# The back half of the delta rule for two groups of heads, 8 matrices, at once

## The chip, the cores and the metric

The kernel runs on one core of a Trainium2 chip. Its metric is device time in microseconds; before, the median of three runs is 2629.19 us (2629.15 to 2630.71). The engines are TensorE (PE in the trace; its weight loads are PEld), VectorE (DVE), ScalarE (ACT), GpSimd (POOL) and SyncE (SP), each with its own instruction stream that runs in program order; they wait for each other by semaphores.

## The reference, cut to what matters

The trunk has two layers over 256 tokens of width 2048 in float32: a gated DeltaNet mixer and MLP, then an indexer-sparse attention and MLP. The change is in the first mixer. In the reference it is, for each of 32 heads and each chunk of tokens:

```python
l_mat = where(strict, (k * beta) @ k.T * decay, 0)
t_mat = triangular_solve(eye + l_mat, eye)          # (1 + L)^-1
u, w = t_mat @ (v * beta), t_mat @ (k * beta * exp(gc))
v_new = u - w @ state
o = (q * exp(gc)) @ state + where(lower, q @ k.T * decay, 0) @ v_new
o = rms_norm(o, out_norm) * silu(z)                 # the norm and the gate
return o.reshape(b, t, 4096) @ w_out
```

## The kernel before, in words

The kernel holds tokens in two blocks of 128 instead of the reference's chunks of 64. A head has one matrix L of 128x128 for each block; the second block takes a correction from the first.

**Main work.** Every weight is loaded by SyncE in items of 512 KB, and `Stream.get` splits each item into two float32r parts (`whi` by ScalarE, `wlo` by VectorE), three items ahead of its use. A product is three matmuls (`mm3`). For each of 16 groups `g` (two value heads, one key head) the main loop makes the projection of k, q, v (`by_channel`, 192 matmuls of 128x256), then that of the gate z (`by_token`, 96 more). After the 16 groups, `two_chunks` starts the output projection, which leaves the last four heads to its end.

**Background work.** The delta rule of a group is a generator, `delta(g, s, zg)`, of some 30 dependent steps. The front half makes convolution, SiLU, the products `pk` of k with k and q, and the masked matrices `la`. The back half is:
- `Lc`, `Lm`, `Tc`, `Tct`: diagonal blocks of 32, inverted by doubling in four levels (lines 599 to 612). A level is a run of 32x32 matmuls, a ScalarE copy to `Pm`, a second run, and VectorE's subtraction and transpose.
- two merges, from blocks of 32 to 64 (32x32 matmuls, lines 617 to 636) and from 64 to 128 (64x64 matmuls, `T64`, `P64`, lines 638 to 646), into `Tt`.
- solve, correction and solve (`r`, `yv`, lines 649 to 665), and the output `o` (lines 667 to 677).
- the norm: four small VectorE steps on `so`, then the inverse root `f` as 13 small GpSimd instructions (line 687); the gate (line 691), four transposes (`aux<-wide,r`), and the split into `hT` (line 700), which marks ("o", 2g) and ("o", 2g+1) as ready.

**What sets the order.** The order on each engine is fixed when the program is built. `Background` interleaves: after each three or four products of the main work `tick` emits steps of at most three active generators, each when a rough account of the engines' times (`Pace`) says that its inputs should be there. `ensure(key)` is the exception: while a key is not ready it emits the oldest generator's steps one after the other, with no main work between them. It stands at line 350 and 370 (an input of the next matmul), at 707, and before the gate tile `zg`, of which there are three:

```python
713            if g > 2:
714                ensure(("o", 2 * g - 6))
```

A generator also waits by itself: line 534 holds `pk` back until the output of group g-2 is ready, since the tiles have two buffers.

On TensorE every float32 matmul is two records in the trace, and a transpose is one; the order below shows instructions, so a run of 16 there is 32 records.

Of the kernel before, what the change touches and what calls it, by code (L numbers as in the profile page):

```python
# [7 lines left out]
F32 = mybir.dt.float32  # L8
F32R = mybir.dt.float32r
I32 = mybir.dt.int32  # L10
AF = mybir.ActivationFunctionType
# [3 lines left out]
P = 128  # L15
# [12 lines left out]
class Pace:  # L28
    """A rough account of when each engine gets through what it has been given, in microseconds."""
# [98 lines left out]
class Stream:  # L128
    """The weights in the order of their use: loaded, and split into two float32r parts, ahead of it."""
# [40 lines left out]
def tile_hybrid_trunk(ctx: ExitStack, tc: tile.TileContext, a: dict, out: bass.AP):  # L170
# [170 lines left out]
    def by_channel(n_items, part, key, n_ct=4, ahead=0):  # L341
        """Channels on partitions: [128 channels, 256 tokens] each, two to a bank."""
# [16 lines left out]
    def by_token(n_items, part, key, n_cols=512, outs=None, k0=0):  # L359
        """Tokens on partitions: [128 tokens, n_cols] for each of the two blocks of tokens."""  # L360
# [17 lines left out]
    def two_chunks(tiles, key, nk):  # L378
        """The first two blocks of columns of a mixer's output, which leave the last heads to the end."""
# [78 lines left out]
    with tc.tile_pool(name="delta", bufs=2, reuse_waits="tile") as dp:  # L458
        gl_dram = dramp.tile([DN_H, T], F32, name="gl_dram")

# [40 lines left out]
        def delta(g, s, zg):  # L501
# [32 lines left out]
            while g > 1 and ("o", 2 * g - 4) not in ready:  # L534
                yield
# [23 lines left out]
            units = [(i, b) for i in range(2) for b in range(2)]  # L559
            line = lambda x: x.rearrange("p i b c -> p (i b c)")  # L560
            rows = lambda q, n=1: slice(B * q, B * (q + n))
            Lc = dp.tile([P, 4, B], F32, name="Lc")
            Lm = dp.tile([P, len(LEVELS), 4, B], F32, name="Lm")
            Tc = dp.tile([P, 4, B], F32, name="Tc")
            Tct = dp.tile([P, 4, B], F32, name="Tct")
            Pm = dp.tile([P, 4, B], F32, name="Pm")
            Tt = dp.tile([P, 2, 2, P], F32, name="Tt")
            pool.memset(Tt, 0.0)
            la = (dp.tile([P, 2, 2, T], F32, name="la0"), dp.tile([P, 2, 2, P], F32, name="la1"))
            for b, n, o in ((0, T, 0), (1, P, T)):  # L570
                for i in range(2):
                    e = E[:, i, o:o + n].unsqueeze(1).to_broadcast([P, 2, n])
                    dve.scalar_tensor_tensor(la[b][:, i], e, wj[:, 2 * i + b:2 * i + b + 1], pk[b], op0=OP.mult, op1=OP.mult)
            for b in range(2):
                for q in range(4):
                    act.copy(Lc[rows(q), b::2], la[b][rows(q), :, 0, rows(q)])
# [6 lines left out]
            r = dp.tile([P, 2, 2, P], F32, name="r")  # L583
            for b in range(2):
                act.activation(r[:, :, b], t[:, :, b], AF.Copy, scale=nk[:, b:b + 1])
# [4 lines left out]
            each = lambda x: x.unsqueeze(1).to_broadcast([P, 4, B])  # L590
# [3 lines left out]
            dve.transpose(Tc.rearrange("p u c -> p (u c)"), Tct.rearrange("p u c -> p (u c)"))  # L594
            pool.tensor_tensor(Lm, Lc.unsqueeze(1).to_broadcast([P, n_l, 4, B]),
                               fine[:, 2:].unsqueeze(2).to_broadcast([P, n_l, 4, B]), op=OP.mult)
            yield True
            small_bank = lambda: aux()[:, 0:4 * B].rearrange("p (u c) -> p u c", u=4)
            for n in range(n_l):
                t = small_bank()  # L600
                for u in range(4):
# [5 lines left out]
                for u in range(4):  # L607
# [3 lines left out]
                dve.transpose(Tct.rearrange("p u c -> p (u c)"), Tc.rearrange("p u c -> p (u c)"))  # L611
                yield
            fold = Lm.rearrange("p n u c -> p (n u c)")
            T64 = fold[:, 0:256].rearrange("p (u c) -> p u c", u=4)
            P64 = fold[:, 256:512].rearrange("p (u c) -> p u c", u=4)
            Ttu = Tt.rearrange("p i b c -> p (i b) c")
            t = small_bank()
            for u, (i, b) in enumerate(units):
# [11 lines left out]
            for u in range(4):  # L630
# [7 lines left out]
            t = aux()[:, 0:256].rearrange("p (u c) -> p u c", u=4)  # L638
            for u, (i, b) in enumerate(units):
# [3 lines left out]
            t = aux()[:, 0:256].rearrange("p (u c) -> p u c", u=4)  # L643
            for u in range(4):
# [3 lines left out]
            # y = T r, with what the first block takes from the second's r  # L648
            yv = dp.tile([P, 2, 2, P], F32, name="yv")
# [10 lines left out]
            for i in range(2):  # L660
                pe.matmul(t[:, i * P:i * P + P], lhsT=la[0][:, i, 0, P:T], rhs=yv[:, i, 0], start=True, stop=True)
            dve.tensor_tensor(r[:, :, 1], r[:, :, 1], t[:, :T].rearrange("p (i d) -> p i d", i=2), op=OP.subtract)
# [3 lines left out]
            # o, its norm and its gate  # L666
            t = aux().rearrange("p (i b d) -> p i b d", i=2, b=2)
            for i in range(2):
                pe.matmul(t[:, i, 0], lhsT=la[0][:, i, 1, 0:P], rhs=yv[:, i, 0], start=True, stop=True)
                pe.matmul(t[:, i, 1], lhsT=la[0][:, i, 1, P:T], rhs=yv[:, i, 0], start=True, stop=False)  # L670
                pe.matmul(t[:, i, 1], lhsT=la[1][:, i, 1, :], rhs=yv[:, i, 1], start=False, stop=True)
            so = small_tile(4, "so")
            o = fold.rearrange("p (i b c) -> p i b c", i=2, b=2)
            act.copy(line(o), line(t))
            for i, b in units:
                act.activation(yv[:, i, b], o[:, i, b], AF.Square, accum_out=so[:, 2 * i + b:2 * i + b + 1])
            yield
            sc = small_tile(2, "sc")
            s2 = small_tile(2, "s2")
            f = small_tile(4, "f")  # L680
            pair = lambda x: x.rearrange("p (i b) -> p i b", i=2)
            rep = lambda x: x.unsqueeze(1).to_broadcast([P, 2, 2])
            dve.tensor_scalar(sc, rs[:, 2:4], 0.25 * float(P ** -0.5), None, op0=OP.mult)
            dve.scalar_tensor_tensor(s2, sc, 4.0 / P, sc, op0=OP.mult, op1=OP.mult)
            dve.tensor_tensor(pair(so), pair(so), rep(s2), op=OP.mult)
            dve.tensor_scalar(so, so, EPS, None, op0=OP.add)
            rsqrt(f, so, 4, pool)
            pool.tensor_tensor(pair(f), pair(f), rep(sc), op=OP.mult)
            yield True
            for i, b in units:  # L690
                dve.scalar_tensor_tensor(r[:, i, b], o[:, i, b], f[:, 2 * i + b:2 * i + b + 1], zg[:, b, i * P:i * P + P],
                                         op0=OP.mult, op1=OP.mult)
            yield
            t = aux()
            for i, b in units:
                pe.transpose(t[:, (2 * i + b) * P:(2 * i + b + 1) * P], r[:, i, b], ident)
            if g % 2 == 0:
                hT.append(h_pair())
            at = slice(2 * (g % 2), 2 * (g % 2) + 2)
            split(t, hT[g // 2][0][:, at].rearrange("p n t -> p (n t)"), hT[g // 2][1][:, at].rearrange("p n t -> p (n t)"), vec("out"))  # L700
            ready.update({("o", 2 * g), ("o", 2 * g + 1)})
# [33 lines left out]
    def chunk_done(outs, c, key, gain, scale=None, last=True):  # L735
        """A block of 512 columns of the residual stream; where it is final, what the next layer takes."""
# [62 lines left out]
    with tc.tile_pool(name="dsa", bufs=1, reuse_waits="tile") as sp, ExitStack() as late:  # L799
# [15 lines left out]
        def q_latent():  # L815
            # 1/sqrt(mean(q^2) + eps) of q = rstd*u is rsqrt(mean(u^2) + eps/rstd^2)/rstd
# [228 lines left out]
```

## Time and profile before

| | |
|---|---|
| median of 3 runs | 2629.19 us |
| profiled execution, span | 2626.4 us |
| TensorE busy | 2588.8 us (99%) |
| VectorE busy | 1546.4 us (59%) |
| ScalarE busy | 1292.3 us (49%) |
| GpSimd busy | 331.1 us (13%) |
| DeltaNet layer, about | 60 to 860 us of the span |
| idle time of TensorE there, named waits | 1.5, 1.0, 0.7, 0.6 and 0.3 us |

The profiled execution's own time is its span; what lies around it in a timed run is taken as the difference to the median, 2.8 us. A busy share says how long an engine had an instruction in it, and TensorE's matmuls overlap, so that its share is read with the spacing of the starts. Times in the timeline are from the span's start, and "x32" means that 32 instructions in a row of one kind are one line.

### The profile page before, as it was taken

The page shows a single profiled execution, that of the slowest core. Times are in us where ns is not written, and L with a number is a line of the kernel's source. Part 1 is how long each engine was busy: PE and PEld are TensorE (multiplying, and loading weights), DVE is VectorE, ACT ScalarE, POOL GpSimd, SP SyncE. Part 2 cuts the span into 40 slices and gives each one's busy share as a digit, 9 for nine tenths or more (in the row PEclk, how much of TensorE's full clock was granted, in tenths as well). Part 3 has the DMA queues.
Part 4 walks back from the last instruction along what each step waited for, and adds up shares of the span by engine and source line. Part 5 has one row for each costly group of instructions (what it writes and reads, how often), then busy time and mean ns, then how long its engine had stood idle before and what let it go on. Part 6 is the DMA issues. An engine that isn't in the chain of part 4 may idle for free.

```text
span 2626.4 us, 52946 instructions
## 1 busy us (share of the span) xinstructions
PE 2588.8 (99%) x21827; PEld 2362.0 (90%) x21827; DVE 1546.4 (59%) x2313; ACT 1292.3 (49%) x1995; POOL 331.1 (13%) x674
## 2 busy tenths in 40 slices
PE   7999999999999999999999999999999999999997
PEld 7999999999987899988899988898899988999886
DVE  5777676676764555554455554586555544455544
ACT  4555555555554444443344444566544433444443
POOL 0344444343431000000000000000000000000000
PEclk9999999999999999999999999999999999999999
DMA  6655455555554566666666666643666666666664
GB/s 191 186 147 141 137 150 139 149 146 147 144 168 153 182 189 195 194 193 193 193 186 186 190 190 188 181 133 120 179 191 194 193 195 194 189 188 187 192 193 137
DMA packets 325394, 455.95 MB, mean 174 GB/s; under 512 B 18280, under 2 KB 159840, under 8 KB 324768
## 3 DMA queue, kind: packets, MB, share of 16 engines
q1 hardware_dynamic: 321888, 443.85, 56.8%
q10 hardware_dynamic: 2928, 7.37, 0.8%
q8 instruction: 171, 2.80, 0.4%
q0 software_dynamic: 336, 1.34, 0.1%
q14 instruction: 71, 0.58, 0.1%
HBM read 450.37 MB, written 2.13 MB: 172 GB/s over the span
## 4 chain that ended last, share of the span: by engine, by line
PE 66%; DVE 1%; ACT 0%; issue 0%; ACTq 0%; DVEq 0%
PE acc L78 64%; PE aux L78 1%; PE pk L78 1%; DVE wlo L78 0%; DVE score L78 0%; ACT whi L78 0%; DVE p L78 0%; DVE m L78 0%; ACT acc L78 0%; DVE qtl L78 0%; DVE nm L78 0%; ACT h L78 0%; DVE h L78 0%; DVE rs_t L78 0%; DVE rs_u L78 0%
## 5 line engine op out<-in xcount | busy, mean ns | idle before, releaser
L78 DVE TENSOR_TENSOR wlo<-raw,whi 128x1024 fp32r<-128x1024 f32 x842 | 1029.6, 1229 | 868.4 <-ACT whi L78 861.3
L78 ACT CAST whi<-raw 128x1024 fp32r<-128x1024 f32 x842 | 878.3, 1049 | 853.3 <-PE acc L78 820.7
L78 PE MATMUL acc<-whi,h 128*128 128x512 f32 x2816 | 886.0, 392 | 2.1 <-ACT acc L78 2.1
L78 PE MATMUL acc<-xhi,whi 128*128 128x256 f32 x3088 | 875.9, 284 | 0.3 <-ACT whi L78 0.3
L78 PE MATMUL acc<-xhi,wlo 128*128 128x256 f32 x3088 | 860.5, 279 | 0.5 <-DVE wlo L78 0.5
L78 PE MATMUL acc<-xlo,whi 128*128 128x256 f32 x3088 | 860.8, 279 | 0.0
L78 PEld LDWEIGHTS acc<-whi,h 128*128 128x128 f32 x2816 | 528.7, 188 | 112.2 <-ACT acc L78 2.9
L78 PEld LDWEIGHTS acc<-xhi,wlo 128*128 128x128 f32 x3088 | 585.1, 189 | 0.8 <-DVE wlo L78 0.8
L78 PEld LDWEIGHTS acc<-xhi,whi 128*128 128x128 f32 x3088 | 581.3, 188 | 4.6 <-ACT whi L78 0.7
L78 PEld LDWEIGHTS acc<-xlo,whi 128*128 128x128 f32 x3088 | 581.8, 188 | 0.2
L78 PE MATMUL acc<-wlo,h 128*128 128x512 f32 x1408 | 548.3, 389 | 0.0
L78 PEld LDWEIGHTS acc<-wlo,h 128*128 128x128 f32 x1408 | 264.5, 188 | 52.7
L78 PE MATMUL acc<-whi,xhi 128*128 128x256 f32 (+2 forms) x576 | 173.6, 301 | 0.0
L78 PE MATMUL acc<-whi,xlo 128*128 128x256 f32 (+2 forms) x576 | 166.4, 289 | 0.0
L78 PE MATMUL acc<-wlo,xhi 128*128 128x256 f32 (+2 forms) x576 | 166.1, 288 | 0.0
L78 POOL DMA_DIRECT2D gain<-in_norm_final x1 | 0.6, 639 | 973.2 <-issue 973.2
L78 DVE SCALAR_TENSOR_TENSOR y<-s,cw,y 128x255 f32<-128x255 f32 (+2 forms) x192 | 93.8, 489 | 40.5 <-ACT y L78 36.0
L78 POOL TENSOR_SCALAR E<-R,tokc 128x128 f32<-128x128 f32 x96 | 86.3, 911 | 247.6 <-DMA R<-gl_dram 144.7
L78 PEld LDWEIGHTS acc<-whi,xhi 128*128 128x128 f32 x576 | 108.0, 187 | 3.6
L78 POOL TENSOR_TENSOR h<-h,gain 128x512 f32<-128x512 f32 x8 | 10.1, 1283 | 790.5 <-ACT acc L78 790.5
L78 PEld LDWEIGHTS acc<-wlo,xhi 128*128 128x128 f32 x576 | 108.3, 188 | 1.3
L78 PEld LDWEIGHTS acc<-whi,xlo 128*128 128x128 f32 x576 | 108.1, 188 | 1.2
(239 smaller groups left out, 1955.9 us busy)
## 6 DMA issues: line engine op xcount, KB each, us to landing
raw<-in_mlp_w_up SPq DMA_DIRECT2D x256, 512.0 KB, 4.3
raw<-in_mlp_w_down SPq DMA_DIRECT2D x256, 512.0 KB, 4.3
raw<-in_dn_w_in SPq DMA_DIRECT2D x66, 512.0 KB, 4.1
raw<-in_dn_w_in SPq DMA_DIRECT2D x256, 128.0 KB, 2.9
raw<-in_dn_w_in SPq DMA_DIRECT2D x128, 256.0 KB, 3.3
raw<-in_dn_w_out SPq DMA_DIRECT2D x64, 512.0 KB, 3.8
raw<-in_dsa_w_out SPq DMA_DIRECT2D x32, 512.0 KB, 3.7
raw<-in_dsa_w_uq SPq DMA_DIRECT2D x16, 512.0 KB, 4.2
```

What stands on the lines that cost most here:

```text
L78: r = f(*args, **kwargs)
```

## The change

The front half stays one generator for each group. The tiles `la` and `r` of two groups (a pair `p` = g // 2) are one tile each, with a single buffer, and the back half is a new generator, `solved`, which runs behind the second group's front half, for four heads of two blocks, 8 matrices. Each of its runs holds twice as many matmuls, and each copy, subtraction and transposition on ScalarE and VectorE, and each GpSimd instruction, twice as many columns. The output and the transposes are two runs each, as a bank holds four matrices. `pk` of either group of a pair waits for all outputs of the pair before. `ensure(("o", 2 * g - 6))` is unchanged. Comments and docstrings go too; they make no instruction.

```diff
-            while g > 1 and ("o", 2 * g - 4) not in ready:
+            while g > 1 and ("o", 4 * (g // 2) - 1) not in ready:
                 yield
...
-            Lc = dp.tile([P, 4, B], F32, name="Lc")
-            Lm = dp.tile([P, len(LEVELS), 4, B], F32, name="Lm")
...
-            pool.memset(Tt, 0.0)
-            la = (dp.tile([P, 2, 2, T], F32, name="la0"), dp.tile([P, 2, 2, P], F32, name="la1"))
+            p, j = g // 2, g % 2
+            if j == 0:
+                pairs[p] = dict(la=(dp.tile([P, 4, 2, T], F32, name="la0", bufs=1), dp.tile([P, 4, 2, P], F32, name="la1", bufs=1)),
+                                r=dp.tile([P, 4, 2, P], F32, name="r", bufs=1), rs=[], zg=[])
+            st_ = pairs[p]
+            la, r = st_["la"], st_["r"]
+            st_["rs"].append(rs)
+            st_["zg"].append(zg)
+            mine = slice(2 * j, 2 * j + 2)
...
             ready.add(("v", g))
-            # (1 + L)^-1 by doubling its diagonal blocks. ...
+            if j == 1:
+                yield from solved(p, **st_)
+
+        def solved(p, la, r, rs, zg):
+            H, U = range(4), [(i, b) for i in range(4) for b in range(2)]
+            n_u = len(U)
...
+            one = lambda shape, name: dp.tile([P] + shape, F32, name=name, bufs=1)
+            Lc, Tc, Tct, Pm = (one([n_u, B], n) for n in ("Lc", "Tc", "Tct", "Pm"))
...
             for n in range(n_l):
                 t = small_bank()
-                for u in range(4):
+                for u in range(n_u):
                     for q in range(4):
                         pe.matmul(t[rows(q), u], lhsT=Lm[rows(q), n, u], rhs=Tc[rows(q), u], start=True, stop=True)
                 act.copy(Pm, t)
                 yield
                 t = small_bank()
-                for u in range(4):
+                for u in range(n_u):
                     for q in range(4):
                         pe.matmul(t[rows(q), u], lhsT=Tct[rows(q), u], rhs=Pm[rows(q), u], start=True, stop=True)
...
             def solve(b):
                 t = aux()
-                for i in range(2):
+                for i in H:
                     pe.matmul(t[:, i * P:i * P + P], lhsT=Tt[:, i, b], rhs=r[:, i, b], start=True, stop=True)
-                act.copy(yv[:, :, b], t[:, :T].rearrange("p (i d) -> p i d", i=2))
+                act.copy(yv[:, :, b], heads(t))
...
+            so = small_tile(8, "so")
+            o = fold.rearrange("p (i b c) -> p i b c", i=4, b=2)
+            for j in range(2):
+                t = aux().rearrange("p (i b d) -> p i b d", i=2, b=2)
+                for i in range(2):
+                    h_ = 2 * j + i
+                    pe.matmul(t[:, i, 0], lhsT=la[0][:, h_, 1, 0:P], rhs=yv[:, h_, 0], start=True, stop=True)
+                    pe.matmul(t[:, i, 1], lhsT=la[0][:, h_, 1, P:T], rhs=yv[:, h_, 0], start=True, stop=False)
+                    pe.matmul(t[:, i, 1], lhsT=la[1][:, h_, 1, :], rhs=yv[:, h_, 1], start=False, stop=True)
+                act.copy(o[:, 2 * j:2 * j + 2].rearrange("p i b c -> p (i b c)"), t.rearrange("p i b d -> p (i b d)"))
+                for u, (i, b) in list(enumerate(U))[4 * j:4 * j + 4]:
+                    act.activation(yv[:, i, b], o[:, i, b], AF.Square, accum_out=so[:, u:u + 1])
+                yield
...
-            rsqrt(f, so, 4, pool)
+            rsqrt(f, so, 8, pool)
...
+            hT.append(h_pair())
+            for j in range(2):
+                t = aux()
+                for n, (i, b) in enumerate(U[4 * j:4 * j + 4]):
+                    pe.transpose(t[:, n * P:n * P + P], r[:, i, b], ident)
...
+                ready.update({("o", 4 * p + 2 * j), ("o", 4 * p + 2 * j + 1)})
+                if j == 0:
+                    yield
```

On TensorE, in before, of group 5's back half: `acc<-whi,xhi` and its like are the main work, `aux<-Tt,Lm` the second 64x64 run, `aux<-wide,s` the next group's value transposes and `aux<-r,Tt` the first solve.

```order
L78 MATMUL aux<-Tt,Lm 64x64 x4
L78 MATMUL acc<-whi,xhi 128x256
L78 MATMUL acc<-wlo,xhi 128x256
L78 MATMUL acc<-whi,xlo 128x256
...
L78 MATMUL aux<-wide,s 128x128 x4
L78 MATMUL acc<-whi,xhi 128x256
...
L78 MATMUL aux<-r,Tt 128x128 x2
L78 MATMUL acc<-whi,xhi 128x256
```

In the change, at the end of the projections of group 5, the same engine has:

```order
L78 MATMUL aux<-Tt,Lm 64x64 x8
L78 MATMUL aux<-r,Tt 128x128 x4
L78 MATMUL aux<-yv,la_2707 128x128 x4
L78 MATMUL aux<-r,Tt 128x128 x4
L78 MATMUL aux<-yv,la_2707 128x128 x2
L78 MATMUL aux<-yv,la_2708 128x128
...
L78 MATMUL aux<-wide,r 128x128 x4
L78 MATMUL acc<-xhi,whi 128x256
```

Where 36 and 6 main matmuls stood between the steps, none stands now: this piece is emitted by `ensure(("o", 2 * g - 6))`, from the first 64x64 run to the first four transposes.

On ScalarE, in before, the same steps (`Lm<-aux 64x256` answers the first 64x64 run, `Tt<-aux` the second, `yv<-aux` the solve) stand among casts of weights:

```order
L78 CAST whi<-raw 128x1024
L78 COPY Lm<-aux 64x256
L78 COPY Lc<-la_4792 32x2x32 x4
L78 COPY Lc<-la_4793 32x2x32 x4
L78 CAST whi<-raw 128x1024
L78 ACTIVATE Tt<-aux 64x4x64
L78 CAST whi<-raw 128x1024
L78 ACTIVATE r<-aux,nk 128x2x128 x2
L78 CAST whi<-raw 128x1024
L78 COPY yv<-aux 128x2x128
L78 ACTIVATE zg<-acc 128x256 x2
L78 CAST whi<-raw 128x1024
```

In the change ScalarE has, at the end of the projections of group 5:

```order
L78 ACTIVATE Tt<-aux 32x8x32 x2
L78 COPY Lm<-aux 64x512
L78 ACTIVATE Tt<-aux 64x8x64
L78 COPY yv<-aux 128x4x128 x2
L78 COPY Lm<-aux 128x512
L78 ACTIVATE yv,so<-Lm 128x128 x4
L78 COPY Lm<-aux 128x512
L78 ACTIVATE yv,so<-Lm 128x128 x4
L78 ACTIVATE h<-aux,vecs 128x512
L78 ACTIVATE zg<-acc 128x256 x2
L78 CAST whi<-raw 128x1024
```

No cast of a weight stands between the steps of this piece; the next one is behind the gate tile.

## Rows read from the trace of the kernel before

**Rows 1.** Busy time of each engine in one stretch of the DeltaNet layer.

```profile
core 0 of [0], span 2626.4 us
core 0: us, PE busy (x) PEld busy (x) DVE busy (x) ACT busy (x) POOL busy (x), PEclk, DMA share, GB/s
400.00:500.00 100.00, 100.00 (x1375) 94.21 (x1375) 69.14 (x155) 56.47 (x122) 42.28 (x90) 1.00 0.52 144
```

**Rows 2.** TensorE's timeline: start, length, engine, line, operation, names, shape, count.

```profile
417.24 0.60 PE L78 MATMUL aux<-r,Tt 128*128 128x128 f32 x4
...
440.71 0.28 PE L78 MATMUL acc<-xhi,wlo 128*128 128x256 f32 x1
440.92 0.45 PE L78 MATMUL aux<-Tc,Lm 32*32 32x32 f32 x32
...
441.52 0.28 PE L78 MATMUL acc<-xlo,whi 128*128 128x256 f32 x1
441.64 0.28 PE L78 MATMUL acc<-xhi,wlo 128*128 128x256 f32 x1
```

**Rows 3.** TensorE's groups by shape, 60 to 860 us: busy us, mean ns.

```profile
L78 PE MATMUL aux<-Tc,Lm 32*32 32x32 f32 x2048 | 29.0, 194 | 0.6 <-DVE Tc L78 0.6
L78 PE MATMUL aux<-r,Tt 128*128 128x128 f32 x128 | 20.6, 284 | 0.0
...
L78 PE MATMUL aux<-Lm,la 64*64 64x64 f32 x128 | 10.8, 224 | 0.0
```

**Rows 4.** Timeline of TensorE and ScalarE about a solve.

```profile
424.93 0.71 PE L78 MATMUL aux<-r,Tt 128*128 128x128 f32 x4
...
425.68 0.37 ACT L78 COPY yv<-aux 128x256 f32<-128x256 f32 x1 [0.34 <-PE aux L78]
```

**Rows 5.** ScalarE's timeline: output copy and the last of four squares.

```profile
429.01 0.59 ACT L78 COPY Lm<-aux 128x512 f32<-128x512 f32 x1 [2.55 <-PE aux L78]
...
430.73 0.19 ACT L78 ACTIVATION_READ_ACCUMULATOR yv<-Lm 128x1 f32 x1
```

**Rows 6.** VectorE's instructions on tile h, 60 to 900 us: ns min/median/max.

```profile
L78 DVE TENSOR_TENSOR h<-acc,h x4: 681/681/684, 857.3 to 859.1; 128x512 f32<-128x512 f32 x4
```

**Rows 7.** VectorE's timeline, from the norm to the gate.

```profile
434.31 0.16 DVE L78 TENSOR_TENSOR so<-so,s 128x4 f32<-128x4 f32 x1
...
434.92 0.17 DVE L78 TENSOR_SCALAR f<-rs_t 128x4 int32<-128x4 int32 x1
...
441.92 1.27 DVE L78 SCALAR_TENSOR_TENSOR r<-Lm,f,zg 128x128 f32<-128x128 f32 x4 [0.65 <-POOL f L78]
```

**Rows 8.** GpSimd's timeline, first and last of the inverse root's 13 instructions.

```profile
435.17 0.20 POOL L78 TENSOR_TENSOR rs_u<-f 128x4 f32<-128x4 f32 x1 [5.73 <-DVE f L78]
...
441.68 0.20 POOL L78 TENSOR_TENSOR f<-f,sc 128x4 f32<-128x4 f32 x1
```

**Rows 9.** GpSimd's and VectorE's timeline in the last group's inverse root.

```profile
837.17 0.20 POOL L78 TENSOR_SCALAR rs_u<-rs_u 128x4 f32<-128x4 f32 x1
...
838.52 1.23 DVE L78 TENSOR_TENSOR wlo<-raw,whi 128x1024 fp32r<-128x1024 f32 x1 [1.49 <-ACT whi L78]
838.58 1.23 POOL L78 TENSOR_TENSOR f<-f,rs_u 128x4 f32<-128x4 f32 x1
```

**Rows 10.** TensorE's timeline at the start of the main work.

```profile
19.64 0.58 PE L78 MATMUL acc<-xhi,wlo 128*128 128x256 f32 x1 [0.47 <-DVE wlo L78]
...
24.07 0.41 PE L78 MATMUL acc<-xhi,wlo 128*128 128x256 f32 x1
24.29 0.39 PE L78 MATMUL acc<-xhi,whi 128*128 128x256 f32 x1
```

**Rows 11.** TensorE's last matmul, and busy time and granted clock behind it.

```profile
2611.89 0.39 PE L78 MATMUL acc<-whi,h 128*128 128x512 f32 x1
...
2612.50:2616.00 3.50, 0.00 (x0) 0.00 (x0) 2.57 (x6) 1.32 (x4) 2.48 (x2) 0.89 0.00 0
2616.00:2620.00 4.00, 0.00 (x0) 0.00 (x0) 2.84 (x11) 1.78 (x2) 0.00 (x0) 0.50 0.14 56
```

More of the change, by code (lines that the diff above doesn't have):

```diff
@@ L459, in tile_hybrid_trunk @@
         gl_dram = dramp.tile([DN_H, T], F32, name="gl_dram")
+        pairs = {}
         def decays(ps):
@@ L572, in delta @@
                     e = E[:, i, o:o + n].unsqueeze(1).to_broadcast([P, 2, n])
[L573 to L576, printed above, removed]
+                    dve.scalar_tensor_tensor(la[b][:, 2 * j + i], e, wj[:, 2 * i + b:2 * i + b + 1], pk[b], op0=OP.mult, op1=OP.mult)
             ready.add(("la", g))
@@ L582, in delta @@
                     pe.transpose(t[:, i, b], s[:, 2 + i, b * P:b * P + P], ident)
-            r = dp.tile([P, 2, 2, P], F32, name="r")
             for b in range(2):
-                act.activation(r[:, :, b], t[:, :, b], AF.Copy, scale=nk[:, b:b + 1])
+                act.activation(r[:, mine, b], t[:, :, b], AF.Copy, scale=nk[:, b:b + 1])
             yield
             ready.add(("v", g))
-            each = lambda x: x.unsqueeze(1).to_broadcast([P, 4, B])
+            if j == 1:
[3 more added lines that the diff above has]
+            n_u = len(U)
+            rows = lambda q, n=1: slice(B * q, B * (q + n))
+            flat = lambda x: x.rearrange("p u c -> p (u c)")
+            one = lambda shape, name: dp.tile([P] + shape, F32, name=name, bufs=1)
+            Lc, Tc, Tct, Pm = (one([n_u, B], n) for n in ("Lc", "Tc", "Tct", "Pm"))
+            Lm = one([len(LEVELS), n_u, B], "Lm")
+            Tt = one([4, 2, P], "Tt")
+            pool.memset(Tt, 0.0)
+            for b in range(2):
+                for q in range(4):
+                    act.copy(Lc[rows(q), b::2], la[b][rows(q), :, 0, rows(q)])
+            each = lambda x: x.unsqueeze(1).to_broadcast([P, n_u, B])
             n_l = len(LEVELS)
@@ L629, in delta @@
             t = small_bank()
-            for u in range(4):
+            for u in range(n_u):
                 pe.matmul(t[rows(1), u], lhsT=Tct[rows(1), u], rhs=Pm[rows(1), u], start=True, stop=True)
@@ L642, in delta @@
             yield
-            t = aux()[:, 0:256].rearrange("p (u c) -> p u c", u=4)
-            for u in range(4):
+            t = small_bank(2 * B)
+            for u in range(n_u):
                 pe.matmul(t[rows(0, 2), u], lhsT=P64[rows(2, 2), u], rhs=Ttu[rows(2, 2), u, rows(2, 2)], start=True, stop=True)
@@ L647, in delta @@
             yield
-            yv = dp.tile([P, 2, 2, P], F32, name="yv")
+            yv = one([4, 2, P], "yv")
+            heads = lambda x: x.rearrange("p (i d) -> p i d", i=4)
             def solve(b):
                 t = aux()
-                for i in range(2):
+                for i in H:
                     pe.matmul(t[:, i * P:i * P + P], lhsT=Tt[:, i, b], rhs=r[:, i, b], start=True, stop=True)
-                act.copy(yv[:, :, b], t[:, :T].rearrange("p (i d) -> p i d", i=2))
+                act.copy(yv[:, :, b], heads(t))
             solve(0)
@@ L659, in delta @@
             t = aux()
-            for i in range(2):
+            for i in H:
                 pe.matmul(t[:, i * P:i * P + P], lhsT=la[0][:, i, 0, P:T], rhs=yv[:, i, 0], start=True, stop=True)
-            dve.tensor_tensor(r[:, :, 1], r[:, :, 1], t[:, :T].rearrange("p (i d) -> p i d", i=2), op=OP.subtract)
+            dve.tensor_tensor(r[:, :, 1], r[:, :, 1], heads(t), op=OP.subtract)
             yield
@@ L665, in delta @@
             yield
[L667 to L683, printed above, removed]
+            so = small_tile(8, "so")
@@ L684, in delta @@
+            sc = small_tile(4, "sc")
+            s2 = small_tile(4, "s2")
+            f = small_tile(8, "f")
+            four = lambda x: x.rearrange("p (j i b) -> p j i b", j=2, i=2)
+            rep = lambda x: x.rearrange("p (j b) -> p j b", j=2).unsqueeze(2).to_broadcast([P, 2, 2, 2])
+            for j in range(2):
+                dve.tensor_scalar(sc[:, 2 * j:2 * j + 2], rs[j][:, 2:4], 0.25 * float(P ** -0.5), None, op0=OP.mult)
             dve.scalar_tensor_tensor(s2, sc, 4.0 / P, sc, op0=OP.mult, op1=OP.mult)
-            dve.tensor_tensor(pair(so), pair(so), rep(s2), op=OP.mult)
+            dve.tensor_tensor(four(so), four(so), rep(s2), op=OP.mult)
@@ L686, in delta @@
             dve.tensor_scalar(so, so, EPS, None, op0=OP.add)
-            rsqrt(f, so, 4, pool)
-            pool.tensor_tensor(pair(f), pair(f), rep(sc), op=OP.mult)
+            rsqrt(f, so, 8, pool)
+            pool.tensor_tensor(four(f), four(f), rep(sc), op=OP.mult)
             yield True
-            for i, b in units:
-                dve.scalar_tensor_tensor(r[:, i, b], o[:, i, b], f[:, 2 * i + b:2 * i + b + 1], zg[:, b, i * P:i * P + P],
+            for u, (i, b) in enumerate(U):
+                dve.scalar_tensor_tensor(r[:, i, b], o[:, i, b], f[:, u:u + 1], zg[i // 2][:, b, (i % 2) * P:(i % 2) * P + P],
@@ L692, in delta @@
                                          op0=OP.mult, op1=OP.mult)
             yield
[L694 to L701, printed above, removed]
+            hT.append(h_pair())
@@ new lines, in solved @@
+            for j in range(2):
+                t = aux()
+                for n, (i, b) in enumerate(U[4 * j:4 * j + 4]):
+                    pe.transpose(t[:, n * P:n * P + P], r[:, i, b], ident)
+                at = slice(2 * j, 2 * j + 2)
+                split(t, hT[p][0][:, at].rearrange("p n t -> p (n t)"), hT[p][1][:, at].rearrange("p n t -> p (n t)"), vec("out"))
+                ready.update({("o", 4 * p + 2 * j), ("o", 4 * p + 2 * j + 1)})
+                if j == 0:
+                    yield
```

27 lines of the change are left out of this document (10 added, 17 removed).

## The prediction

> **What bounds the kernel now.** I read the busy table by stretch first: in a stretch of the DeltaNet layer TensorE is busy 100.00 of 100.00 us, VectorE 69.14, ScalarE 56.47, GpSimd 42.28, at a granted clock of 1.00 [rows 1]. So in this layer the time is TensorE's instruction stream, and the price of every small matmul run is what it adds to that stream; work on the other engines is free while it ends before TensorE needs it. Then the TensorE timeline, to see what a run of small matmuls costs between the large ones; then the timelines of the engines that answer such a run; last the order of the changed kernel, to see whether large matmuls still stand between the steps of the chain.
>
> **The change part by part.**
>
> *Fewer, longer runs (a gain).* A run of 32 records of 32x32 for one group stands between two large matmuls: from the start of the last one ahead (440.71) to the start of the second behind (441.52) are 0.81 us, where two large ones alone take 2 x 0.115 (the next pair of starts is 0.12 apart). The run costs 0.58 [rows 2]. Its records start (0.45 - 0.194) / 31 = 0.008 us apart [rows 2, 3], so that 32 more in the same run add 0.26, and the second run's entry, 0.58 - 0.26 = 0.32, is saved. Ten such runs go per pair of groups: eight of the doubling, two of the first merge (16 and 24 records, which I price alike). Eight pairs: 80 x 0.32 = 25.6 us. The 64x64 runs I price at 0.3 by the same row. In the first and the last pair two of four go: 2 x 2 x 0.3 = 1.2. In the six pairs between all four leave the large matmuls, and what takes their place is counted as idle below: 6 x 4 x 0.3 = 7.2. Gain: 34.0 us. For the 128x128 runs I count nothing: their four records fill their time.
>
> *The shorter instruction lists of VectorE, ScalarE and GpSimd (nothing).* About half as many, twice as wide. TensorE's full stream hides them today and gains nothing by their going.
>
> *A longer answer within a level (nothing, up to 11.5 us).* In the doubling, 12 large matmuls (1.4 us) stand between the two runs of a level, before and now. The first run is 0.26 longer and the copy behind it at most 0.1, by the wider copies on record (0.37 for 256 columns, 0.59 for 512) [rows 4, 5]. TensorE was never short there, so a level is late by 0 to 0.36; 32 levels give 0 to 11.5 us. I take 0, since the stretch shows no idle time at all [rows 1], and keep the other end.
>
> *The wait that the change adds.* Before group g's gate tile, `ensure(("o", 2g-6))` emits steps of the oldest chain until that output is there, with no large matmul between them. In before the chain of group g-3 is long through. Now that output comes from a pair, whose back half starts only after its second group's front half; and the first `pk` of the next pair waits for the whole of it. The order says where this ends. From one pair's first `pk` stand 234 large matmuls to its second, 150 more to the first doubling run, and 162 on the second merge run has been reached; 6 later the next odd group's projection ends, and everything that is left of the chain follows in one piece: first 64x64 run, second, solve, correction, solve, two outputs, transposes. So for groups 5, 7, 9, 11, 13 and 15; for group 3 the piece starts at the second solve; for the last pair, where the output projection needs its last heads, at the second output. Eight stalls. Behind the waiting instruction on TensorE stand all matmuls of the next group; three weight items are split ahead, so nothing else is late there afterwards. No DMA is added: the weight loads on SyncE and the `R` loads on ScalarE's queue stand behind the same tiles as before, and a stall lets the loads run ahead.
>
> The price is TensorE's idle time in such a piece. From a run's last record to ScalarE's start: the record (0.284 for 128x128, 0.224 for 64x64) [rows 3] and 0.05 (424.93 + 0.71 = 425.64 to 425.68) [rows 4]; the same 0.05 I take for the way back. ScalarE's copies are now 512 columns wide, 0.59 as its 128x512 copy [rows 5]. A 128x128 record's own slot is (0.60 - 0.284) / 3 = 0.105 [rows 2, 3].
> - 64x64, twice: 0.22 + 0.05 + 0.59 + 0.05 = 0.91 each, 1.82.
> - first solve: 0.28 + 0.05 + 0.59 + 0.05 - 0.11 = 0.86.
> - correction, on VectorE from PSUM at 512 columns (0.68) [rows 6]: 0.95.
> - second solve: 0.86, less four records (0.42) that don't need it: 0.44.
> - output to transposes. From the second solve's copy: 8 records 1.02, 0.05, then ScalarE's copy and four squares for either half, 430.73 + 0.19 - 429.01 = 1.91, twice; 4.89. TensorE has issued its 20 records by 2.1. VectorE's four small steps are 0.2 apart (434.31 to 434.92) [rows 7], 0.81 with two handoffs 0.91. GpSimd's inverse root: 13 instructions 0.282 apart when nothing holds them (837.17 to 838.58 are five) [rows 9]: 3.67. A handoff, the first gated product (1.27 / 4 = 0.32) [rows 7] and a handoff: 0.42. First transpose at 9.89, idle 7.8; the other three transposes come at VectorE's 0.32 instead of 0.105: 0.6. Together 8.4.
>
> Sum 12.5 us; six times 75. Group 3: 0.44 + 8.4 = 8.8. The last pair has only its second half open: 0.28 + 0.05 + 1.91 + 0.91 + 3.67 + 0.42 + 0.6 - 0.1 = 7.7. Idle: 91.5 us.
>
> *The inverse root, weighed.* Beside the other work it took 6.71 us, 435.17 to 441.88 [rows 8], and single instructions of it grow from 0.20 to 1.23 just while VectorE makes a weight part of 1.23 [rows 9]. In the stall the order has no weight part, so I take 3.67; the other end is 6.71. The Trainium skill (SBUF — State Buffer, Who interferes with whom) says that VectorE with two SBUF inputs and GpSimd share a port pair held for a whole instruction, the other "fully blocks". The trace agrees, 1.23 beside 1.23; by that rule the chain is 3.67 in the stall, and were it not so, 6.71.
>
> *The clock.* TensorE's last matmul ends at 2612.28, and the mean granted clock is 0.89 in the 3.5 us from 2612.5 and 0.50 in the 4 us after [rows 11]: it fell to 1.2 GHz at about 2615.2, some 2.9 us after the engine stopped. The 7.8 us before the transposes are longer. What a fall costs is seen at the start: dense from 19.64 to 24.29, at starts 0.22 apart instead of 0.115 [rows 2, 10], 4.65 us in which 2.2 are lost. I take 2 us for each of eight, 16; the ends are 0 (the clock holds) and 18. The Trainium skill (TensorE: Matmul & The Clock Gate, What's actually happening) has it that "the default state is throttled, and activity releases the throttle"; by it the 16 stand, without it the sum is 16 less.
>
> Sum on the profiled execution: 2626.4 [rows 1] + 91.5 - 34.0 + 16 = 2699.9. The median of the runs, 2629.19, is 2.8 above that span; so 2702.7, **2703 us**.
>
> **The rivals.**
> *The clock holds.* All else the same: 2703 - 16 = 2687. For it: TensorE works until 7.8 us before, in short bursts. Against it: the end of the trace.
> *GpSimd's chain stays blocked.* 8 x (6.71 - 3.67) = 24: 2727; with late levels 2739. For it: it has been so beside TensorE's dense stream. Against it: no weight part stands there.
> *The other side: the runs decide, and the forced piece costs nothing.* Then 34.0 us are gained, 2595. It needs each of eight stalls, with its clock, under 34.0 / 8 = 4.2 us. For it: today's chain always came in time, without idle time of TensorE. Against it: GpSimd's chain alone has 3.67 and the squares 3.8, and the order has no large matmul to put beside them. The Trainium skill (TensorEngine Tiling (Array Packing), PSUM Bottleneck) advises to read several tiles of a bank at once, and its Key Properties say that a change of tiling drains the engine; the 0.32 of entry agrees with that, and by these two rules alone the change comes out at 2595.
> That the change doesn't do what it says is excluded by the order: the runs have doubled, from 32 records to 64.
>
> **How the numbers follow.** My forecast, with clock falls and a free GpSimd chain: 0.66, with 2690 to 2715. The clock holds: 0.16. GpSimd stays blocked or levels are late: 0.12. The other side: 0.03. Stalls and gain about even: 0.03. 2676 to 2738 takes in the first three with some us for the handoffs, which I have only in the one direction. A difference of 0.2%, 5 us, is what a measurement of this kernel can tell from none; so slower 0.94, within 0.02, faster 0.04.
>
> **What would show it.** In the profile after: eight stretches, about 100 us apart, in which TensorE's busy share falls; its waits naming VectorE's gated product (some 8 x 7 us) and ScalarE's copies under 1 us each; starts of large matmuls 0.21 apart behind the transposes and a granted clock under 1.00 there; GpSimd's 13 instructions in about 3.7 us; runs of 64 records at about 0.84 us. The forecast is wrong if TensorE waits for less than 4 us in a pair of groups, or if the waits lie in the doubling instead.

## The result, and the profile after

The changed kernel takes 2724.93 us (median of 4 runs, 2718.45 to 2731.8) against 2629.17 (2629.05 to 2630.71) of the kernel before: a ratio of 1.0362, 95% interval 1.0347 to 1.0377. Forecast were 2703 us and a range of 2676 to 2738. So the direction, the place and the range were as said; the time was 22 us longer than forecast, and that has causes of its own below. The changed kernel's four runs spread over 13 us, and the mean granted clock goes with them: 0.981 in the shortest, 0.975 in the longest.

The busy table of one stretch of the DeltaNet layer, from behind one stall to behind the next, against the 100.00 of 100.00 in [rows 1]:

```profile
core 0: us, PE busy (x) PEld busy (x) DVE busy (x) ACT busy (x) POOL busy (x), PEclk, DMA share, GB/s
199.00:301.00 102.00, 91.25 (x1282) 87.13 (x1281) 64.11 (x120) 49.58 (x91) 35.63 (x62) 0.97 0.47 130
```

TensorE now stands still for 10.75 us of it, and its mean granted clock is 0.97. The named waits of TensorE from 60 to 960 us (who waits, for whom, us in total, times, longest) tell what it waits for:

```profile
PE aux L78 <- DVE r L78: 67.0, 14, 9.6
PE aux L78 <- ACT yv L78: 4.7, 9, 0.7
PE aux L78 <- ACT Lm L78: 4.6, 6, 0.8
PE aux L78 <- ACT Tt L78: 4.1, 6, 0.7
```

`r` is VectorE's gated product (and, six times for 0.78, its correction). Before, the waits in this layer were 1.5 us and less. The second pair's forced piece on TensorE's timeline, with nothing of the main work between its rows, up to the first three large matmuls behind it:

```profile
279.01 1.14 PE L78 MATMUL aux<-Lm,la 64*64 64x64 f32 x16
280.91 1.11 PE L78 MATMUL aux<-Tt,Lm 64*64 64x64 f32 x16 [0.76 <-ACT Lm L78]
282.70 1.16 PE L78 MATMUL aux<-r,Tt 128*128 128x128 f32 x8 [0.68 <-ACT Tt L78]
284.54 1.16 PE L78 MATMUL aux<-yv,la 128*128 128x128 f32 x8 [0.68 <-ACT yv L78]
286.48 1.16 PE L78 MATMUL aux<-r,Tt 128*128 128x128 f32 x8 [0.78 <-DVE r L78]
...
288.31 2.50 PE L78 MATMUL aux<-yv,la 128*128 128x128 f32 x20 [0.23 <-ACT yv L78]
298.41 1.17 PE L78 MATMUL aux<-wide,r 128*128 128x128 f32 x4 [7.60 <-DVE r L78]
...
299.23 0.56 PE L78 MATMUL acc<-xhi,whi 128*128 128x256 f32 x1
299.59 0.41 PE L78 MATMUL acc<-xlo,whi 128*128 128x256 f32 x1
299.81 0.41 PE L78 MATMUL acc<-xhi,wlo 128*128 128x256 f32 x1
```

From its first row to the first large matmul behind it are 20.2 us, and behind it the second and third start 0.22 apart. In the piece GpSimd's inverse root, first and last of its 13 instructions (6.71 us in [rows 8]):

```profile
294.27 0.20 POOL L78 TENSOR_TENSOR rs_u<-f 128x8 f32<-128x8 f32 x1 [18.97 <-DVE f L78]
...
297.67 0.20 POOL L78 TENSOR_TENSOR f<-f,sc 128x8 f32<-128x8 f32 x1
```

From 294.27 to 297.87 are 3.60 us. The next pair's piece has the same rows, but here solve and correction take 2.08 where they took 1.16, and the last 24 output records 4.08 (the same view):

```profile
384.42 2.08 PE L78 MATMUL aux<-r,Tt 128*128 128x128 f32 x8 [0.68 <-ACT Tt L78]
387.17 2.08 PE L78 MATMUL aux<-yv,la 128*128 128x128 f32 x8 [0.68 <-ACT yv L78]
...
391.89 4.08 PE L78 MATMUL aux<-yv,la 128*128 128x128 f32 x24
403.57 1.17 PE L78 MATMUL aux<-wide,r 128*128 128x128 f32 x4 [7.59 <-DVE r L78]
```

The granted clock (the number behind POOL's) in both pieces:

```profile
286.00:292.00 6.00, 4.10 (x32) 3.72 (x32) 0.73 (x4) 2.92 (x11) 0.00 (x0) 1.00 0.00 0
292.00:298.00 6.00, 0.00 (x0) 0.00 (x0) 0.78 (x5) 1.28 (x8) 2.61 (x13) 0.77 0.00 0
...
386.00:392.00 6.00, 4.54 (x20) 3.96 (x19) 1.00 (x4) 0.59 (x1) 0.00 (x0) 0.50 0.00 0
392.00:397.00 5.00, 3.97 (x25) 3.66 (x24) 0.00 (x0) 2.75 (x11) 0.00 (x0) 0.77 0.00 0
395.00:396.00 1.00, 0.97 (x9) 0.78 (x7) 0.00 (x0) 0.97 (x5) 0.00 (x0) 1.00 0.00 0
397.00:401.50 4.50, 0.00 (x0) 0.00 (x0) 0.68 (x4) 1.44 (x9) 1.48 (x8) 0.95 0.00 0
401.50:408.00 6.50, 4.43 (x21) 4.29 (x22) 3.74 (x12) 2.28 (x4) 1.13 (x6) 0.51 0.00 0
```

In the first the clock falls once, in the gap before the transposes, as forecast. In the second it is at 1.2 GHz from about 384, is back at 2.4 GHz by 395, while the 24 output records still run, and falls again at about 401. That is so in four of the six full pieces, which are 23.7 to 24.0 us long, from the last large matmul ahead to the first behind; the two others are 20.4. Last, a run of 64 records between large matmuls, for [rows 2]:

```profile
352.11 0.28 PE L78 MATMUL acc<-xhi,wlo 128*128 128x256 f32 x1
352.32 0.75 PE L78 MATMUL aux<-Tc,Lm 32*32 32x32 f32 x64
...
353.23 0.29 PE L78 MATMUL acc<-xlo,whi 128*128 128x256 f32 x1
```

From 352.11 to 353.23 are 1.12, less 0.23 for two large ones: 0.89, where two runs of 32 cost 2 x 0.58.

### The profile page after: what moved, and what is told of

Its sections match the earlier page's. It is cut to its first block, busy times and chain, and to the rows that moved or that the text cites. A ratio compares the mean times of both kernels' runs of the same rounds, so it can differ in the third digit from the quotient of the medians.

```text
span 2722.5 us, 52422 instructions
## 1 busy us (share of the span) xinstructions
PE 2600.5 (96%) x21827; PEld 2381.5 (87%) x21827; DVE 1539.2 (57%) x2161; ACT 1266.7 (47%) x1827; POOL 297.7 (11%) x514
## 4 chain that ended last, share of the span: by engine, by line
PE 64%; DVE 1%; ACT 0%; issue 0%; ACTq 0%; DVEq 0%
PE acc L78 62%; PE aux L78 1%; PE pk L78 1%; DVE wlo L78 0%; DVE score L78 0%; ACT whi L78 0%; ACT h L78 0%; DVE p L78 0%; DVE m L78 0%; ACT acc L78 0%; DVE h L78 0%; DVE qtl L78 0%; DVE nm L78 0%; DVE rs_t L78 0%; DVE rs_u L78 0%
## 5 line engine op out<-in xcount | busy, mean ns | idle before, releaser
L78 POOL TENSOR_SCALAR E<-R,tokc 128x128 f32<-128x128 f32 x96 | 108.8, 1147 | 113.3 <-DMA raw<-in_dn_w_in 80.9
```

What stands on the lines that cost most here:

```text
L78: r = f(*args, **kwargs)
```

## The experiments

Each is a variant of the changed kernel. Two theories stood at the start. *The loop:* a pair's chain is longer than the two groups projected beside it, because the next pair's first `pk` waits for the whole of it (one set of `la` and `r`) and group g asks for the output of group g-3 (three gate tiles). *One cause alone:* either of the two suffices.

### e1_gate: a fourth gate tile

```diff
-            if g > 2:
-                ensure(("o", 2 * g - 6))
-            zg = dp.tile([P, 2, T], F32, name="zg", bufs=3)
+            if g > 3:
+                ensure(("o", 2 * g - 8))
+            zg = dp.tile([P, 2, T], F32, name="zg", bufs=4)
```

(`Pm` takes the place of `Lc`, for room.)

> The changed kernel with a fourth buffer for the gate tile, so that group g asks for the outputs of group g-4 instead of g-3. Theory: the chain of a pair is longer than the two groups that are projected beside it, and the first pk of the next pair waits for all of it; so the forced piece only moves, to the next place where group g asks for work of the pair (the v of group g-2). By the order of TensorE, the 64x64 runs, both solves and the correction then have 12 large matmuls between them again, and only the stretch from the outputs to the transposes stays bare, in five pairs (8.4 us each, and one fall of the clock, 2 us); the last pair's whole back half becomes bare (12.5 + 4), the one before it half (5 + 2). Idle 5 x 8.4 + 12.5 + 5 = 59.5, clock 16, gain of the longer runs 96 x 0.28 = 27: 2626.4 + 59.5 + 16 - 27 = 2675 on the span, about 2677. Rival, the number of gate buffers alone is the cause: no stall but the last, about 2610.

Measured: 2721.77 us, 1.035 of the kernel before (1.0336 to 1.0365): 3 us less than the changed kernel, within the spread of its runs, and 45 above the theory. The kind was as the theory had it, the size was not. TensorE's waits in the layer:

```profile
PE aux L78 <- DVE r L78: 52.3, 8, 7.6
PE pk L78 <- DVE s L78: 13.1, 6, 2.4
PE aux L78 <- DVE Tc L78: 7.8, 11, 1.8
```

The stretch from outputs to transposes stayed bare, with 7.6 each. What I had missed: the second `pk` of a pair was now forced as well and waited about 2 us for VectorE's `s` (13.1), and the last pair had its whole inverse bare, 46.6 us without a large matmul (889.57 to 936.12), at a granted clock of 0.50 from 896 to 924, where TensorE was busy for 19.03 of 28 us. A wait that is taken from one place of a loop that is too long comes back at others.

### e2_double: two sets of la and r

```diff
-            while g > 1 and ("o", 4 * (g // 2) - 1) not in ready:
+            while g > 3 and ("o", 4 * (g // 2) - 5) not in ready:
```

The even pairs' `la` and `r` lie in four tiles of the pool of `hT`; `solved` waits for the pair before it.

> The changed kernel with two sets of la and r, so that the first pk of a pair waits for the pair before the last; the gate tile keeps three buffers. Theory: the steps of a pair then come up to two groups' length earlier, so that when group g asks for the outputs of group g-3 the chain stands at the second solve instead of the first 64x64 run; the stretch from outputs to transposes is bare in pairs 0 to 6 (8.4 us and a 2 us fall of the clock each), partly in the last (4 + 2). Idle 63, clock 16, gain 27: 2626.4 + 52 = 2678 on the span, about 2681; TensorE's waits for ScalarE's copies in the bare piece are gone, the one for VectorE's gated product stays at about 7 us, seven times. Rival, the single set of la and r alone is the cause: no bare piece but the last, about 2610.

Measured: 2691.96 us, 1.024 (1.0224 to 1.0256): 11 us above the theory, far from the rival. TensorE's waits:

```profile
PE aux L78 <- DVE h L78: 30.1, 4, 7.5
PE aux L78 <- DVE r L78: 26.6, 4, 7.5
PE aux L78 <- ACT Pm L78: 6.1, 7, 0.9
PE aux L78 <- DVE Tc L78: 2.7, 7, 0.4
```

The gated product (`h` or `r`, by pair) has its 7.5 in pairs 0 to 6, the first rows of the piece are gone; new are waits within the doubling, 6.1 + 2.7 against 0.5 + 1.5 in the changed kernel, and 4.8 us in which TensorE waited for nothing that the profile names.

### e3_both: both edits

> Both edits at once: four gate buffers, two sets of la and r. Theory: by the order of TensorE at least 12 large matmuls stand between any two steps of every chain and 78 or more between outputs and transposes, but for the last pair, which has 24 there (2.8 of 9.9 us). So seven of eight stalls and their clock go, and what stays of the change is the gain of the longer runs: 96 x 0.28 = 27 us less, 7 + 2 for the last pair: 2626.4 - 27 + 9 = 2608 on the span, about 2611 (2605 to 2618): faster than the kernel before by 0.7%. Rival one, each wide step is late in the stream too (32 levels of the doubling at up to 0.36, and ScalarE's wider copies): 2611 + 12 = 2623. Rival two, the runs gain nothing: 2638.

Measured: 2629.13 us (11 runs), 0.9999 (0.999 to 1.0008). Neither edit alone removes the stalls, both together remove seven of eight: the loop theory holds. But of the gain of 18 us that I had forecast nothing is left. TensorE's waits:

```profile
PE aux L78 <- DVE Tc L78: 8.4, 7, 1.8
PE aux L78 <- DVE r L78: 7.7, 1, 7.7
```

7.7 were expected for the last pair. The 8.4 are rival one: a doubling step that comes late in the stream. In the longest of these waits its VectorE step stands behind three convolution products and a weight part of the next group (VectorE's timeline, TensorE's row that waits, and the busy time and clock behind it):

```profile
330.07 1.63 DVE L78 SCALAR_TENSOR_TENSOR y<-s,cw,y 128x255 f32<-128x255 f32 x3
331.62 1.22 DVE L78 TENSOR_TENSOR wlo<-raw,whi 128x1024 fp32r<-128x1024 f32 x1
332.75 0.41 DVE L78 TENSOR_TENSOR Tc<-Tc,aux 128x256 f32<-128x256 f32 x1
...
333.22 0.75 PE L78 MATMUL aux<-Tc,Lm 32*32 32x32 f32 x64 [1.78 <-DVE Tc L78]
...
334.60:338.00 3.40, 3.40 (x77) 3.11 (x76) 3.29 (x6) 1.32 (x2) 0.00 (x0) 0.53 0.64 170
```

Behind this wait of 1.78 the clock was at 0.53 from 334.6 to 338.0, with TensorE busy all through. So it was behind the one of 1.77 at 518.40 (0.52 from 519.0 to 522.4), but not behind those of 1.49 and 1.73 at 246.85 and 607.69. So it stands at equal: 19.4 us more of named waits than before (23.5 from 60 to 960 us against 4.1) and some us of clock, against what the runs bring, which by this difference is about 25. That is a remainder, not a measurement; e9_halves tests the price of entering a run by itself.

### e4_keep: TensorE kept busy in the stalls

```diff
+            keep(3)      # behind each of four steps; keep(n): n matmuls 128x512
...
+            keep(32)     # ahead of the norm
             sc = small_tile(4, "sc")
```

> The changed kernel with matmuls added that read a tile of the projections' input and whose results nobody reads: three 128x512 behind each of four steps of the back half, 32 in the gap before the norm. They keep TensorE busy in the stalls, so that its clock should not fall. Theory: the falls cost 31 us in the changed kernel (more than the 16 of the prediction, since in four stalls the clock falls twice), and the sums of the idle times are as before: 2722.5 - 31 + 5 (the added matmuls in the first and last pair, where they stand in the stream) = 2697 on the span, about 2699. Rival, the falls cost 16 as predicted and the rest lies in longer waits: about 2714. Granted clock 1.00 in all stalls by both.

Measured: 2706.73 us, 1.0293 (1.0279 to 1.0307): 18 us less than the changed kernel by the medians, 22.0 by the two profiled executions (2700.5 and 2722.5). The theory had 25.5 and the rival 11, so the profiled executions speak for the theory; the medians lie about midway. Busy times and clock in its second piece:

```profile
287.00:293.00 6.00, 5.60 (x40) 4.82 (x39) 0.95 (x4) 2.64 (x11) 0.00 (x0) 1.00 0.01 3
293.00:300.50 7.50, 7.19 (x34) 5.45 (x32) 1.99 (x9) 1.56 (x9) 2.61 (x13) 1.00 0.00 0
```

The clock stays at 2.4 GHz, all six pieces take 20.5 us (20.4 in the changed kernel where the clock held), so the added matmuls cost nothing there, and the steps of the chain are as long as before. Without the stalls' clock, then, the change would still cost some 66 us: 2700.5 - 2626.4 = 74.1, less about 8 for the added matmuls that do cost time and for a fall that is left (both below).

### e5_dve: the inverse root on VectorE

```diff
-            rsqrt(f, so, 8, pool)
-            pool.tensor_tensor(four(f), four(f), rep(sc), op=OP.mult)
-            yield True
+            rsqrt(f, so, 8)
+            dve.tensor_tensor(four(f), four(f), rep(sc), op=OP.mult)
+            yield
```

> The changed kernel with the 13 instructions of the inverse root on VectorE instead of GpSimd. Theory: in the bare piece every step adds up, and GpSimd's share can be replaced one for one. In the changed kernel VectorE's gated product starts 3.95 us behind VectorE's last small step (293.96 to 297.91); with 13 steps 0.205 apart on VectorE itself it would be 14 x 0.205 = 2.87, so 1.08 less in each of eight stalls, 8.6 us: about 2716. TensorE's wait for the gated product falls from 7.6 to 6.5. Rival, GpSimd's chain is hidden by something else that ends as late (the squares, a weight part): no change, 2725.

Measured: 2711.33 us, 1.0313 (1.0299 to 1.0327): 13.6 less, not 8.6. VectorE's timeline, the last step before the root and the gated product behind it:

```profile
294.84 0.17 DVE L78 TENSOR_SCALAR f<-rs_t 128x8 int32<-128x8 int32 x1
...
297.13 1.14 DVE L78 SCALAR_TENSOR_TENSOR r<-Lm,f,zg 128x128 f32<-128x128 f32 x4
```

2.29 instead of 3.95, since `rsqrt` needs 10 instructions on VectorE (two operations in one), not the 13 that I had counted: 1.66 in each of eight stalls are 13.3. The root is on the path one for one; the rival is out.

### e9_halves: the runs cut in two again

```diff
                 for u in range(n_u):
+                    if u == 4:
+                        yield
                     for q in range(4):
```

In both runs of each doubling level of e3_both.

> The kernel with both edits (four gate buffers, two sets of la and r, the planner's pause as it was), with every 64-record run of the doubling issued as two runs of 32 records and large matmuls between them: 80 entries more, the chain otherwise as it is. Theory: entering a run costs 0.28 us of TensorE's stream, so 80 x 0.28 = 22 more than with both edits (2629), and about 3 for the last pair, whose back half comes later: 2654, less up to 10 where the chain's steps are no longer late: 2644 to 2654. Rival, the entry is free and the records alone cost: 2629 to 2632.

Measured: 2640.64 us, 1.0042 (1.0029 to 1.0056): 11.5 more than e3_both, under the range. A half run costs what it cost before the change (TensorE's timeline):

```profile
422.73 0.28 PE L78 MATMUL acc<-xhi,wlo 128*128 128x256 f32 x1
422.94 0.45 PE L78 MATMUL aux<-Tc,Lm 32*32 32x32 f32 x32
...
423.55 0.28 PE L78 MATMUL acc<-xlo,whi 128*128 128x256 f32 x1
```

0.82 - 0.23 = 0.59, twice 1.18, against 0.89: 0.29 for each entry. The edit cuts the doubling's runs alone, two in each of four levels of eight pairs, so it adds 64 entries; the 80 that I had expected count the two runs of the first merge too, which stay whole. 64 x 0.29 are 18.6 us. Less came out because the chain is late less often: the named waits from 60 to 960 us are 20.1 against 23.5 in e3_both (the doubling's 4.9 against 8.4), and the two falls of the clock in the stream, 3.4 us each, are gone, at half speed another 3.4 by estimate. 18.6 - 3.4 - 3.4 = 11.8, against 11.5. So the entry has its price, the rival of a free entry is out, and a shorter run is less often late.

### e7_slack, e8_all, e10_last, e11_pause: towards a faster version

The first of these has, over e3_both:

```diff
         for g in range(DN_G):
+            bg.SLACK = 0.8 if g < 12 else 0.2
...
         bg.drain()
+        bg.SLACK = 0.4
```

> The kernel with both edits (four gate buffers, two sets of la and r), and the planner's pause between two steps of a chain set to 0.8 instead of 0.4 for groups 0 to 11 and to 0.2 for the rest. Theory: the kernel with both edits had the gain of the longer runs (27 us) but gave it back: waits in the stream for the doubling's VectorE step (8.4) and for ScalarE's copy (2.3), the falls of the clock behind them, and the last pair's bare piece (7.7 and about 6 of clock). With the longer pause VectorE has room, and the last pair's back half comes some 12 large matmuls of the output projection (2.7 us) earlier against its end: 2629 - 10.7 - 4 - 3 = about 2611. Rival, the runs gain nothing and the waits replace each other: stays at 2629.

Measured: 2629.43 us, 1.0 (0.9991 to 1.0009): my theory fell, and of the rival the part on the waits holds: they replaced each other. Under the pause of 0.8 the doubling's waits shrank to at most 0.77, but the first, of 1.30, at 155; under 0.2 they grew to 3.08 and 2.44.

e8_all is e7_slack with the edit of e5_dve.

> The same, and the inverse root on VectorE. Theory: it shortens only the last pair's bare piece (1.1 to 2 us), and VectorE has room for 13 more small instructions per pair in the stream: 2609. Rival, VectorE's added work makes doubling steps late again: 2615 or more.

Measured: 2622.21 us, 0.9971 (0.9959 to 0.9982): 0.3% under the kernel before and 7.2 us under e7_slack, where 1.1 to 2 were expected. The last pair's wait fell from 6.06 to 2.94; the fall of the clock behind it stayed (0.51 over 7 us in both). Part of the rest came in the stream: the wait at 700 went from 2.44 to 1.32, and the fall behind it is gone (granted clock from 700 to 708: 0.79, now 1.00). Three weight parts (3.49 us) then stood on VectorE ahead of the last gated product; e10_last puts them behind it (no `yield` between root and product in the last pair).

> The fastest so far (both edits, the planner's pause 0.8 and 0.2, the inverse root on VectorE), and in the last pair the gated product is issued right behind the inverse root instead of a step later, ahead of three weight parts on VectorE. Theory: in the fastest so far the last bare piece is 2.94 us of wait, and three weight parts (3.49 us, from 829.99) stand on VectorE between the root's end and the gated product; without them the transposes come where the large matmuls end, the wait goes and the fall of the clock behind it (about 1.5): 2622.2 - 2.9 - 1.5 = 2618. Rival, the weight parts were wanted as early as they stood and now TensorE waits for them: 2622 or more.

Measured: 2622.97 us, 0.9975 (0.9966 to 0.9984): no change, as the rival had it. The wait for `r` is gone, the same three weight parts now hold up the split of the transposes (VectorE, VectorE, and TensorE's row that waits for it):

```profile
833.38 3.49 DVE L78 TENSOR_TENSOR wlo<-raw,whi 128x1024 fp32r<-128x1024 f32 x3
836.79 0.74 DVE L78 SCALAR_TENSOR_TENSOR h<-aux,vecs,h 128x512 fp32r<-128x512 f32 x1
...
837.59 0.79 PE L78 MATMUL acc<-whi,h 128*128 128x512 f32 x1 [3.09 <-DVE h L78]
```

e11_pause keeps 0.8 for one group more (`g < 13`).

> The same, with the longer pause kept for one group more (0 to 12). Theory: in the fastest so far the largest wait in the stream, 2.49 us for a doubling step at 604, and the fall of the clock behind it come where the pause is 0.2 already; under 0.8 such waits were 0.56 to 0.76: 2618 - 2 - 1 = 2615. Rival, the wait only moves to the next pair: 2618.

Measured: 2622.96 us, 0.9978 (0.9969 to 0.9987). The wait at 602 stayed (2.72). By the order that pair's doubling still falls under the pause of 0.2, one group later than I had thought, so that the run doesn't tell the two apart.

## Why the prediction was right, and where it was short

**The place and the mechanism.** Right: six full pieces some 100 us apart, a shorter one ahead and one behind; the longest waits name VectorE's gated product, and those for ScalarE's copies are 0.68 and 0.76. e3_both takes seven of the eight stalls away, and its edits touch nothing but buffers. The range held in part by luck: the inner band of the forecast, 2690 to 2715, was missed, and the measured time lies next to the 2727 of a rival whose mechanism did not occur.

**The idle time.** Right. In the second pair, from the output's remaining records (288.31) to the first transpose (298.41) are 10.10 us, where 9.89 were worked out. The whole piece came out 0.4 us longer than its sum, some 2 us over six.

**GpSimd's root.** Right: 3.60 against 3.67, with no weight part beside it, and e5_dve shows that it counts in full. Of the Trainium skill (SBUF — State Buffer, Who interferes with whom) the trace agrees with what was drawn from it: 3.60 without the large VectorE instruction beside it, 6.71 with it [rows 8, 9].

**The clock.** The step that was mis-sized: I took one fall of 2 us in each of eight stalls, 16 us, from the start of the kernel and its end [rows 10, 11]. In four stalls there were two falls, the first within the piece, while TensorE worked 1.1 of each 1.8 us. Those four pieces are 3.3 to 3.6 us longer, 14 in all; behind the eight stalls large matmuls lose another 15 by their starts, 0.21 apart instead of 0.115. Together some 29. e4_keep comes to about the same by another way: it takes 22.0 us less by the profiled executions, and in it 12 of the added matmuls still cost 12 x 0.23 = 2.8 in the first pair and as much in the last, where the steps have main work between them (32 of them in a row take 7.52), and the last pair keeps a fall that costs about 2.3: 22.0 + 5.6 + 2.3 = 29.9 (26 by the medians). By the 29 this is 13 of the 22 us.

**The longer runs.** A merge saves 2 x 0.58 - 0.89 = 0.27, not 0.32: the run's later records are 0.0097 apart, (0.89 - 0.58) / 32, not 0.008. Over 80 runs the gain is 4 us less than said. e9_halves measures 0.29 for the same entry. The 8.4 us that the 64x64 runs were to save no run measures by themselves.

**The last pair.** 7.7 were worked out; TensorE's rows there:

```profile
936.27 1.17 PE L78 MATMUL aux<-wide,r 128*128 128x128 f32 x4 [9.55 <-DVE r L78]
938.22 0.80 PE L78 MATMUL acc<-whi,h 128*128 128x512 f32 x1 [0.78 <-ACT h L78]
...
945.03 0.50 PE L78 MATMUL acc<-whi,h 128*128 128x512 f32 x1 [0.78 <-ACT h L78]
```

11.1 in all: a weight part (929.61, 1.23) stood on VectorE ahead of the norm, and behind the transposes the output projection waits for their split, which I had left out. Some 3 us more than worked out. So 13 + 4 + 3 + 2 = 22, against 2722.5 - 2699.9 = 22.6 in this one execution.

**The rivals.** The clock that holds is out by the granted clock and by e4_keep, GpSimd's blocked chain by its 3.60 us. The other side, 2595, is a bound of what the change can bring without its stalls (2599 with the entry as measured). The best version with both edits reached 2622: its doubling steps are still late (7.8 us of TensorE's waits), and the last pair keeps a wait of 2.9 and a fall of the clock. The late levels that I priced at 0 to 11.5 and put to 0 were indeed near 0 in the changed kernel, but 8.4 us in e3_both, where the doubling of one pair meets the convolution of the next group; in each of the four waits over 1 us three convolution products stand on VectorE ahead of the step.

## What to carry to other kernels

Before work is batched to be wider, count the loop: how many main instructions lie from one batch's first step to the last one that frees a buffer for the next, and whether that fits into the main work of one batch. If not, this builder forces the rest into one piece; one more buffer moved the stalls (e1_gate) or shortened them (e2_double), and only both together took them away. In such a piece each hop between engines counts in full, and TensorE's clock is a second price, about a third of the idle time here (29 against 91.5 us worked out).

## What had not been expected of the hardware

- TensorE's clock fell to 1.2 GHz while the engine was working in bursts: in four of six pieces of one shape, about at their third row. In the piece shown it was back at 1.00 while the output records still ran (395 to 396) and fell again at about 401. In the other two pieces, alike up to there (starts 1.90 and 1.79 apart; 1.90 and 1.80 in one that fell), it held. In e5_dve the second pair's piece, which kept its clock through the bursts in the changed kernel, was at 0.50 from 280 to 290. The Trainium skill (TensorE: Matmul & The Clock Gate, What's actually happening) says that the chip's watch on the engine's activity is free-running and does not start with the kernel. That pieces alike fall differently agrees with it; no run here shows the watch itself.
- Of four waits of 1.49 to 1.78 us in a dense stream (e3_both) two were followed by 3.4 us at a clock of 0.53 and 0.52, and two by a clock of 1.00. The two that fell, 1.77 and 1.78, are hardly longer than one that did not, 1.73.
- The spacing of 32x32 float32 records in a run was 0.008 to 0.010 us, and entering such a run 0.27 to 0.29 us.
